# Where a wide up-projection's product is transposed, and the rate of wide pieces near the end of a feed-forward block

## The chip, the cores and the metric

The kernel runs on one core of one Trainium2 chip. It is timed in device microseconds (us) of one execution. A core has TensorE (PE; its weight loads are listed apart as PEld), VectorE (DVE), ScalarE (ACT), GpSimd (POOL) and SyncE (SP), which here only issues DMAs. Each engine works through its own queue in order.

## What is computed

Two layers of a decoder trunk on 256 tokens of width 2048, in float32. Each layer has an attention block and then a gated feed-forward block with a layer norm after it. The change touches the feed-forward blocks alone:

```python
SEQ = 256; D_MODEL = 2048; DEPTH = 2; D_FF = 5632

def swiglu(x, w_gate, w_up, w_down):
    return (jax.nn.silu(x @ w_gate) * (x @ w_up)) @ w_down
...
    x = layer_norm(DEEPNORM_ALPHA * x + y, ln_g[layer, 0], ln_b[layer, 0])
    y = swiglu(x, w_gate[layer], w_up[layer], w_down[layer])
    x = layer_norm(DEEPNORM_ALPHA * x + y, ln_g[layer, 1], ln_b[layer, 1])
```

## The kernel before

Float32 products are made of three matmuls each: every operand is split into a high part (`XH`, `wh`, `sh`) and a rest (`XL`, `wl`, `sl`), and high times high, high times rest and rest times high are summed in PSUM.

**Chunks and pieces.** The weights come as chunks of 512 columns, and a chunk as pieces of 256 rows by 512 columns (512 KB). `D_FF` gives 11 blocks of columns, f = 0 to 10. `g0_9` is the gate chunk of layer 0 and block 9, `u0_8` the up chunk of block 8, and `d0_3_2` the third of four down chunks that take in blocks 6 and 7. A chunk of the gate or of up has 8 pieces, and this down chunk has 4. `visits` is the list of pieces in the order in which PE works through them; one entry is a visit. Both layers have the same list.

**Plain and wide pieces.** A plain piece is 12 matmuls of 512 columns. Its load goes to one of four `raw` buffers, ACT writes the high part (line 422) and DVE the rest (line 424). Gate chunks from block 2 on, and the up chunk of block 8 (`UPS`), are wide (`c.S`): `emit_s` multiplies them by a Strassen-like scheme, in 21 matmuls of 256 columns (lines 448 to 450) that read three sums of blocks of the piece. So the split of a wide piece (`split_s`) is longer: three pre-sums on DVE in the raw buffer (lines 380, 382, 383), the high part `sh` on ACT (line 386), the rest `sl` on DVE (line 389). There are two raw buffers for wide pieces (`sraw_92`, `sraw_93`), and two pairs of split buffers (`sh_102` with `sl_103`, `sh_104` with `sl_105`). The raw buffer is free for the next load when line 389 has read it; the pair of split buffers is free when PE has done the piece. The high part and the rest are not put in the queues with the pre-sums: they are owed (`owe`, `pay`), and go in behind a later split.

**The order.** `ffn_part` lays out the plain visits and puts the wide ones between them at a rate: `want` grows by 0.53 per plain visit from the tenth on, and by 0.7 from number 118 on, which is near the end of `u0_7`. After each visit `feed_more` takes in the next splits as buffers allow, in the order of the pieces. When a wide chunk is done, `drain_s` gathers its four accumulators: one pass on ACT (line 478) and five on DVE (lines 479 to 484). For up of block 8, DVE then multiplies by the gate (line 1089).

**Transposes.** The product of block f has to be transposed before the down chunks can use it: `h_T` puts four transposes of 128x128 in one PSUM bank (line 597), twice (t = 0 and 1), and ACT and DVE move each bank to `YH` and `YL` (lines 113 and 114). `after_up[layer, f]` says after which two visits. From block 2 on the banks come from `PAIRS`: the plain chunk in work holds one pair, and the transposes take a bank of the other pair, which the plain chunk before held and the next one will hold. A down chunk's two banks are read by line 928.

Of the kernel before, what the change touches and what calls it, by code (L numbers as in the profile page):

```python
# [53 lines left out]
def trunk_kernel(ctx: ExitStack, tc: tile.TileContext, x, ab_w_in, b_f, ab_w_out,  # L54
# [67 lines left out]
    visits = []  # L122
    chunks = {}

    def add_chunk(name, xs, kslots, srcs, tags=None):
        subs = []
        o = 0
        for n in srcs[0]:
            subs.append((n, o))
            o += n  # L130
        c = Chunk(name, xs, kslots, subs, srcs[1], tags or ("mm",) * len(subs))
        c.n = o
        chunks[name] = c
        return c

    def kmajor(c, hs=None):
        for h in (range(c.nh) if hs is None else hs):
            visits.append((c, h, (0, 1)))
# [18 lines left out]
    def lead_begin(c):  # L157
        for t in (0, 1):
            for h in range(LEAD):
                visits.append((c, h, (t,)))  # L160
        kmajor(c, range(LEAD, c.nh))

    def rows(w, k0, cols):
        return [(o, n, w[k0:k0 + 256, c0:c0 + n].rearrange("(k p) c -> p k c", p=P))
                for o, n, c0 in cols]
# [37 lines left out]
    after_up = {}  # L203
    win = {}

    def ffn_part(layer):
        def wide(nm, w, f):
            return add_chunk(f"{nm}{layer}_{f}", "X", K16, ([512], lambda h: rows(
                w[layer], h * 256, [(0, 512, f * 512)])))

        def down(gi):
            grp = GROUPS[gi]
            slots = [4 * (f % 4) + k for f in grp for k in range(4)]
            for n in range(4):
                c = add_chunk(f"d{layer}_{gi}_{n}", "Y", slots, (
                    [512], lambda h, n=n: rows(
                        w_down[layer], grp[0] * 512 + h * 256, [(0, 512, n * 512)])))
                if gi == len(GROUPS) - 1 and n == 3:
                    (lead_final if layer == 1 else lead_end)(c)
                else:  # L220
                    kmajor(c)

        g0 = wide("g", w_gate, 0)
        g0.pair = 0
        lead_begin(g0)
        base = len(visits)
        for f in range(NF):
            if f == 1:
                kmajor(wide("g", w_gate, 1))
            c = wide("u", w_up, f)  # L230
            if f in UPS:
                c.S = True
            else:
                kmajor(c)
            if f in (1, 3, 5, 7):
                down(f // 2)
        down(len(GROUPS) - 1)
        flat = visits[base:]
        del visits[base:]
        ends = {}  # L240
        for f in range(NF):
            if f not in UPS:
                e = ends[f] = max(k for k, v in enumerate(flat) if v[0].name == f"u{layer}_{f}")
                o = e + 2 - f % 2
                after_up[layer, f] = [(v[0].name, v[1], v[2]) for v in flat[o:o + 3]]
        gates = []
        for f in range(len(PLAIN), NF):
            c = wide("g", w_gate, f)
            c.S = True
            gates += [(c, h, (0, 1)) for h in range(8)]  # L250
            if f in UPS:
                gates += [(chunks[f"u{layer}_{f}"], h, (0, 1)) for h in range(8)]
        near = {ends[f] + 2 for f in (1, 3, 5, 7, 9)}
        ns, want = 0, 0.0
        for k, v in enumerate(flat):
            visits.append(v)
            want = max(want + (0 if k < 9 else 0.53 if k < 118 else 0.7),
                       ns + 1 if k in near else 0)
            while ns < min(len(gates), int(want)):
                visits.append(gates[ns])  # L260
                ns += 1
                c = gates[ns - 1][0]
                f = int(c.name[3:])
                if ns % 8 == 0 and c.name[0] == "g" and f not in UPS:
                    assert k < ends[f] - 1, (k, ns, ends)
        assert ns == len(gates)
        for f in UPS:
            e = max(k for k, v in enumerate(visits) if v[0].name == f"u{layer}_{f}")
            after_up[layer, f] = [(v[0].name, v[1], v[2]) for v in visits[e + 1:e + 3]]

    w_out_part("oa", ab_w_out[0])
    ffn_part(0)
    wi = mla_w_in[0]
    c = add_chunk("m0", "X", K16, ([512], lambda h: rows(wi, h * 256, [(0, 512, 0)])))
# [8 lines left out]
    for nm in order:  # L283
# [8 lines left out]
        kmajor(c)  # L292
    w_out_part("om", mla_w_out[0])
    ffn_part(1)


# [1161 lines left out]
```

## Time and profile before

| | |
|---|---|
| three runs | 2169.24, 2170.62 (median), 2171.04 us |
| the profiled execution | 2170.17 us, its span 2168.3 us |
| PE busy | 2131.5 us, 98% of the span |
| DVE busy | 1639.8 us, 76% |
| ACT busy | 1046.3 us, 48% |
| DMA | 410.39 MB, mean 189 GB/s |
| mean granted TensorE clock | 0.994 |

The span runs from the first instruction to the last; some 1.9 us of the execution lie around it. PE's share is that of modelled ends, so a busy PE isn't yet a PE at its best pace: the start of one matmul to the start of the next tells more. An idle time in brackets is that of the instruction's engine just before it, with what ended it.

### The profile page before, as it was taken

Reading aid. Unit: us, or ns where it says so; the run is one execution under the profiler, and the core shown is the slowest. Engines: PE = TensorE matmul, PEld = TensorE weight load, DVE = VectorE, ACT = ScalarE, POOL = GpSimd, SP = SyncE. Lnnn points to the kernel's source line nnn. Section 1 sums busy time; section 2 is a strip of 40 time slices with the busy share of each in tenths; the row PEclk is TensorE's granted clock in tenths of the full one; section 3 lists DMA queues with packets and bytes.
Section 4 is the critical chain, followed back from the end, with each engine's and each line's share of the span. In section 5 each row is a group of like instructions: output and inputs, shape, how many; then the busy total and the mean of one; then the engine's idle time right before and its main releaser. Section 6 shows DMA issues by size and latency. Waiting matters only on the chain.

```text
span 2168.3 us, 31334 instructions
## 1 busy us (share of the span) xinstructions
PE 2131.5 (98%) x12426; PEld 1865.3 (86%) x12426; DVE 1639.8 (76%) x2117; ACT 1046.3 (48%) x1210; POOL 94.5 (4%) x142
## 2 busy tenths in 40 slices
PE   9999999999999999989999999999999999999998
PEld 9899998788888888878878998878888888887886
DVE  5555656788888888888866676598887888888875
ACT  5444544455444454444534665355544444454451
POOL 2100000100000000000001330010000000000000
PEclk9999999999999999999999999999999999999999
DMA  8565556555565555555765544745654555555582
GB/s 287 170 206 165 172 185 216 192 184 190 169 208 191 194 194 189 183 184 173 258 214 163 176 133 143 274 139 182 204 195 165 187 198 189 198 166 173 200 282 78
DMA packets 230338, 410.39 MB, mean 189 GB/s; under 512 B 14088, under 2 KB 58160, under 8 KB 229168
## 3 DMA queue, kind: packets, MB, share of 16 engines
q1 hardware_dynamic: 230192, 408.40, 56.5%
q8 instruction: 97, 1.59, 0.3%
q14 instruction: 49, 0.40, 0.1%
HBM read 402.56 MB, written 5.78 MB: 188 GB/s over the span
## 4 chain that ended last, share of the span: by engine, by line
PE 59%; issue 35%; DVE 3%; DMA 1%; POOL 1%; ACT 1%; SPq 0%; DVEq 0%; POOLq 0%; ACTq 0%
PE mm L117 12%; PE mm L118 12%; PE mm L119 12%; PE mm L507 3%; PE mm L509 3%; PE mm L511 3%; PE tp L597 2%; PE att L119 1%; PE att L118 1%; PE att L117 1%; PE sA L449 1%; PE sB L449 1%; PE sC L449 1%; PE sC L450 1%; PE sB L448 1%
## 5 line engine op out<-in xcount | busy, mean ns | idle before, releaser
L422 ACT ACTIVATE wh<-raw 128x1024 fp32r<-128x1024 f32 (+3 forms) x424 | 443.0, 1048 | 576.5 <-PE mm L119 358.2
L424 DVE TENSOR_TENSOR wl<-raw,wh 128x1024 fp32r<-128x1024 f32 (+3 forms) x424 | 511.5, 1211 | 193.0 <-ACT wh L422 186.4
L389 DVE TENSOR_TENSOR sl<-sraw,sh 128x1792 fp32r<-128x1792 f32 x160 | 323.5, 2022 | 37.6 <-ACT sh L386 37.4
L117 PE MATMUL mm<-wh,XH 128*128 128x512 f32 (+3 forms) x896 | 350.1, 391 | 0.0
L118 PE MATMUL mm<-wl,XH 128*128 128x512 f32 (+3 forms) x896 | 346.7, 387 | 0.0
L119 PE MATMUL mm<-wh,XL 128*128 128x512 f32 (+3 forms) x896 | 346.0, 386 | 0.0
L117 PE MATMUL mm<-wh,YH 128*128 128x512 f32 (+1 forms) x768 | 306.8, 400 | 11.3 <-DVE YL L114 10.7
L118 PE MATMUL mm<-wl,YH 128*128 128x512 f32 (+1 forms) x768 | 304.7, 397 | 0.0
L119 PE MATMUL mm<-wh,YL 128*128 128x512 f32 (+1 forms) x768 | 304.4, 396 | 0.0
L386 ACT ACTIVATE sh<-sraw 128x1792 fp32r<-128x1792 f32 x160 | 270.3, 1689 | 13.6 <-DVE sraw L383 10.6
L119 PEld LDWEIGHTS mm<-wh,XL 128*128 128x128 f32 x896 | 168.1, 188 | 36.6
L117 PEld LDWEIGHTS mm<-wh,XH 128*128 128x128 f32 x896 | 168.6, 188 | 31.2
L118 PEld LDWEIGHTS mm<-wl,XH 128*128 128x128 f32 x896 | 168.3, 188 | 30.6
L117 PEld LDWEIGHTS mm<-wh,YH 128*128 128x128 f32 x768 | 145.6, 190 | 43.4 <-DVE YL L114 11.4
L119 PEld LDWEIGHTS mm<-wh,YL 128*128 128x128 f32 x768 | 145.2, 189 | 35.2
L118 PEld LDWEIGHTS mm<-wl,YH 128*128 128x128 f32 x768 | 145.4, 189 | 30.7
L380 DVE TENSOR_TENSOR sraw<-sraw 128x512 f32<-128x512 f32 x160 | 109.5, 685 | 12.3 <-DMA sraw<-in_ffn_w_gate_dram 11.8
L507 PE MATMUL mm<-XH,wh 128*128 128x256 f32 x364 | 104.0, 286 | 0.0
L509 PE MATMUL mm<-XH,wl 128*128 128x256 f32 x364 | 102.3, 281 | 0.0
L511 PE MATMUL mm<-XL,wh 128*128 128x256 f32 x364 | 102.2, 281 | 0.0
L448 PE MATMUL sA<-sh,XH 128*128 128x256 f32 x320 | 92.1, 288 | 0.0
L449 PE MATMUL sA<-sl,XH 128*128 128x256 f32 x320 | 89.9, 281 | 1.8 <-DVE sl L389 1.8
(302 smaller groups left out, 4254.2 us busy)
## 6 DMA issues: line engine op xcount, KB each, us to landing
raw<-in_ffn_w_down_dram SPq DMA_DIRECT2D x160, 512.0 KB, 5.5
raw<-in_ffn_w_up_dram SPq DMA_DIRECT2D x155, 512.0 KB, 4.8
sraw<-in_ffn_w_gate_dram SPq DMA_DIRECT2D x149, 512.0 KB, 3.9
raw<-in_ab_w_in_dram SPq DMA_DIRECT2D x80, 256.0 KB, 3.1
raw<-in_ffn_w_gate_dram SPq DMA_DIRECT2D x27, 512.0 KB, 4.5
sraw<-in_ab_w_in_dram SPq DMA_DIRECT2D x48, 256.0 KB, 3.3
raw<-in_ab_w_out_dram SPq DMA_DIRECT2D x22, 512.0 KB, 3.5
sraw<-in_ffn_w_up_dram SPq DMA_DIRECT2D x21, 512.0 KB, 4.0
```

Source lines behind the costliest of these rows:

```text
L117: nc.tensor.matmul(o, lh, rh, start=start, stop=False)
L118: nc.tensor.matmul(o, lh, rl, start=False, stop=False)
L119: nc.tensor.matmul(o, ll, rh, start=False, stop=stop)
L386: nc.scalar.activation(sh, r[:, 256:2048], AF.Copy)
L389: nc.vector.tensor_tensor(sl, r[:, 256:2048], sh.bitcast(F32), op=ALU.subtract)
L422: nc.scalar.activation(wh[:, a:b], r[:, a:b], AF.Copy)
L424: nc.vector.tensor_tensor(wl[:, a:b], r[:, a:b], wh[:, a:b].bitcast(F32), op=ALU.subtract)
L448: nc.tensor.matmul(o, h, w[0][:, q], start=first, stop=False)
L449: nc.tensor.matmul(o, h, w[1][:, q], start=False, stop=False)
L507: nc.tensor.matmul(o, wh[:, kk, a:a + P], XH[:, slot, :], start=first, stop=False)
L509: nc.tensor.matmul(o, wl[:, kk, a:a + P], XH[:, slot, :], start=False, stop=False)
L511: nc.tensor.matmul(o, wh[:, kk, a:a + P], XL[:, slot, :], start=False, stop=last)
```

## The change

Two edits in `ffn_part`. The rate of wide pieces from plain visit 118 on is 0.74 and not 0.7. And `after_up` of block 8, whose up chunk is wide, is taken from the plain visits behind the last piece of that chunk: the first of them that begins a chunk, and the one behind that. Before it was the next two visits, of whatever kind.

```diff
-            want = max(want + (0 if k < 9 else 0.53 if k < 118 else 0.7),
+            want = max(want + (0 if k < 9 else 0.53 if k < 118 else 0.74),
                        ns + 1 if k in near else 0)
             while ns < min(len(gates), int(want)):
                 visits.append(gates[ns])
...
         for f in UPS:
             e = max(k for k, v in enumerate(visits) if v[0].name == f"u{layer}_{f}")
-            after_up[layer, f] = [(v[0].name, v[1], v[2]) for v in visits[e + 1:e + 3]]
+            rest = [v for v in visits[e + 1:] if not v[0].S]
+            o = next(k for k, v in enumerate(rest) if v[1] == 0)
+            after_up[layer, f] = [(v[0].name, v[1], v[2]) for v in rest[o:o + 2]]
```

The visits from the second piece of `u8` on, in either layer, a wide one by its name (u8.1 is piece 1 of `u0_8` or `u1_8`) and a plain one as p:

```
before: u8.1 p u8.2 p p u8.3 p u8.4 p u8.5 p p u8.6 p u8.7 p p g9.0 p g9.1 p p g9.2 p g9.3 p g9.4 p p g9.5 p g9.6 p p g9.7 p g10.0 p p g10.1 p g10.2 p g10.3 p p g10.4 p g10.5 p p g10.6 p g10.7 p p
after:  u8.1 p u8.2 p u8.3 p u8.4 p p u8.5 p u8.6 p p u8.7 p g9.0 p g9.1 p p g9.2 p g9.3 p g9.4 p p g9.5 p g9.6 p g9.7 p p g10.0 p g10.1 p g10.2 p p g10.3 p g10.4 p g10.5 p g10.6 p p g10.7 p p p p
```

The two plain visits behind u8.7 are `d0_3_1` piece 3 and `d0_3_2` piece 0 in both. Before, the transposes stand behind these two. After, they stand behind `d0_3_2` pieces 0 and 1. Up to u8.2 the two lists are the same, and so they are behind the last row above. The same instructions run, in both layers; only their order is another. Lines of the changed kernel from 269 on are two higher.

PE at the first transposes of `u8`'s product, before (`mm_7982` is a bank of `d0_3_1`, `mm_8116` one of `d0_3_2`, `tp` the bank of the transposes, `gt` the product):

```order
L119 MATMUL mm_7982<-wh_96,YL 128x512
L597 MATMUL tp_8103<-ident,gt_3529 128x128 x4
L117 MATMUL mm_8116<-wh_98,YH 128x512
L118 MATMUL mm_8116<-wl_99,YH 128x512
L119 MATMUL mm_8116<-wh_98,YL 128x512
```

The same place after (`mm_8137` is a bank of `d0_3_2`, `sA_8106` an accumulator of `g0_9`):

```order
L119 MATMUL mm_8137<-wh_98,YL 128x512
L599 MATMUL tp_8150<-ident,gt_3529 128x128 x4
L450 MATMUL sA_8106<-sh_104,XH 128x256
L451 MATMUL sA_8106<-sl_105,XH 128x256
L452 MATMUL sA_8106<-sh_104,XL 128x256
```

The transposes stood between the end of one down chunk and the start of the next. Now they stand behind the first piece of that next chunk, and piece 1 of `g0_9` follows.

DVE behind the last piece of `u8`, before (the first row is the last of the drain; `sl_103<-sraw_93` is the rest of g9.0, the pre-sums on `sraw_92` belong to g9.1, the two rows of line 928 read `d0_3_1`):

```order
L484 TENSOR_TENSOR xt_3526<-xt_3526,sC_7690 128x2x256
L1089 TENSOR_TENSOR gt_3529<-gt_3529,xt_3526 128x1024
L380 TENSOR_TENSOR sraw_92<-sraw_92 128x512
L382 TENSOR_TENSOR sraw_92<-sraw_92 128x256
L383 TENSOR_TENSOR sraw_92<-sraw_92 128x256
L389 TENSOR_TENSOR sl_103<-sraw_93,sh_102 128x1792
L424 TENSOR_TENSOR wl_95<-raw_91,wh_94 128x1024
L928 TENSOR_TENSOR X_3525<-X_3525,mm_7981 128x512
L928 TENSOR_TENSOR X_3525<-X_3525,mm_7982 128x512
L114 TENSOR_TENSOR YL<-tp_8103,YH 128x4x128
```

And after:

```order
L486 TENSOR_TENSOR xt_3526<-xt_3526,sC_7689 128x2x256
L1091 TENSOR_TENSOR gt_3529<-gt_3529,xt_3526 128x1024
L382 TENSOR_TENSOR sraw_92<-sraw_92 128x512
L384 TENSOR_TENSOR sraw_92<-sraw_92 128x256
L385 TENSOR_TENSOR sraw_92<-sraw_92 128x256
L391 TENSOR_TENSOR sl_103<-sraw_93,sh_102 128x1792
L426 TENSOR_TENSOR wl_101<-raw_90,wh_100 128x1024
L426 TENSOR_TENSOR wl_95<-raw_91,wh_94 128x1024
L391 TENSOR_TENSOR sl_105<-sraw_92,sh_104 128x1792
L930 TENSOR_TENSOR X_3525<-X_3525,mm_7980 128x512
L930 TENSOR_TENSOR X_3525<-X_3525,mm_7981 128x512
```

The rest of g9.0 keeps its place behind the drain, while PE's visit of g9.0 comes one plain piece earlier. One more plain split and the rest of g9.1 stand ahead of the two rows that free `d0_3_1`'s banks; line 114 comes later.

DVE from the rest of g10.4 (`sl_103<-sraw_93`) to that of g10.5 (`sl_105<-sraw_92`), before; line 114 belongs to transposes:

```order
L389 TENSOR_TENSOR sl_103<-sraw_93,sh_102 128x1792
L424 TENSOR_TENSOR wl_97<-raw_88,wh_96 128x1024
L114 TENSOR_TENSOR YL<-tp_8725,YH 128x4x128
L424 TENSOR_TENSOR wl_99<-raw_89,wh_98 128x1024
L389 TENSOR_TENSOR sl_105<-sraw_92,sh_104 128x1792
```

The same stretch after; line 1087 multiplies `u9` by its gate, and the pre-sums on `sraw_93` are those of g10.6:

```order
L391 TENSOR_TENSOR sl_103<-sraw_93,sh_102 128x1792
L426 TENSOR_TENSOR wl_101<-raw_90,wh_100 128x1024
L1087 TENSOR_TENSOR gt_3530<-gt_3530,mm_8440 128x512
L1087 TENSOR_TENSOR gt_3530<-gt_3530,mm_8441 128x512
L382 TENSOR_TENSOR sraw_93<-sraw_93 128x512
L384 TENSOR_TENSOR sraw_93<-sraw_93 128x256
L385 TENSOR_TENSOR sraw_93<-sraw_93 128x256
L391 TENSOR_TENSOR sl_105<-sraw_92,sh_104 128x1792
```

The rest of g10.5 now stands behind the pre-sums of g10.6, which work in the buffer that the rest of g10.4 has just read. The visits of g10.4 and g10.5 have one plain piece between them in both lists.

## Rows read from the trace of the kernel before

**Rows 1.** The page: busy time, share of the span and instructions of each engine.

```profile
PE 2131.5 (98%) x12426; PEld 1865.3 (86%) x12426; DVE 1639.8 (76%) x2117; ACT 1046.3 (48%) x1210; POOL 94.5 (4%) x142
```

**Rows 2.** Who waited for whom on PE: us in total, times, longest us.

```profile
PE mm L117 <- DVE YL L114: 10.7, 2, 5.7
...
PE sA L449 <- DVE sl L389: 1.8, 4, 0.8
```

**Rows 3.** The timeline of PE, layer 0: start us, us, instruction, count [idle before].

```profile
960.11 0.39 PE L117 MATMUL mm<-wh,YH 128*128 128x512 f32 x1
...
963.00 0.66 PE L597 MATMUL tp<-ident,gt 128*128 128x128 f32 x4
...
969.38 0.80 PE L117 MATMUL mm<-wh,YH 128*128 128x512 f32 x1 [5.73 <-DVE YL L114]
...
974.35 0.60 PE L597 MATMUL tp<-ident,gt 128*128 128x128 f32 x4
...
974.71 0.36 PE L448 MATMUL sA<-sh,XH 128*128 128x256 f32 x1
```

**Rows 4.** The timeline of DVE over the same wait.

```profile
958.97 0.42 DVE L479 TENSOR_TENSOR xt<-xt,sD 128x256 f32<-128x256 f32 x1
...
961.72 1.22 DVE L1089 TENSOR_TENSOR gt<-gt,xt 128x1024 f32<-128x1024 f32 x1
...
964.38 2.02 DVE L389 TENSOR_TENSOR sl<-sraw,sh 128x1792 fp32r<-128x1792 f32 x1
...
966.31 1.22 DVE L424 TENSOR_TENSOR wl<-raw,wh 128x1024 fp32r<-128x1024 f32 x1
...
967.45 1.28 DVE L928 TENSOR_TENSOR X<-X,mm 128x512 f32<-128x512 f32 x2
```

**Rows 5.** The timeline of PE at the same place of layer 1.

```profile
1973.49 0.65 PE L597 MATMUL tp<-ident,gt 128*128 128x128 f32 x4
...
1984.45 0.37 PE L448 MATMUL sA<-sh,XH 128*128 128x256 f32 x1
```

**Rows 6.** Timelines of DVE, SP and PE: g10.1's rest, the load behind it, g10.2.

```profile
1029.65 2.02 DVE L389 TENSOR_TENSOR sl<-sraw,sh 128x1792 fp32r<-128x1792 f32 x1
...
1031.69 0.37 SPq L358 DMA_DIRECT2D sraw<-in_ffn_w_gate_dram  x1
...
1035.74 0.69 DVE L380 TENSOR_TENSOR sraw<-sraw 128x512 f32<-128x512 f32 x1 [2.94 <-DMA sraw<-in_ffn_w_gate_dram]
...
1037.26 2.02 DVE L389 TENSOR_TENSOR sl<-sraw,sh 128x1792 fp32r<-128x1792 f32 x1
...
1039.33 0.39 PE L449 MATMUL sA<-sl,XH 128*128 128x256 f32 x1 [0.31 <-DVE sl L389]
```

**Rows 7.** The timeline of DVE: two rests with two plain splits between them.

```profile
936.70 2.02 DVE L389 TENSOR_TENSOR sl<-sraw,sh 128x1792 fp32r<-128x1792 f32 x1
...
940.90 2.02 DVE L389 TENSOR_TENSOR sl<-sraw,sh 128x1792 fp32r<-128x1792 f32 x1
```

**Rows 8.** Timelines of DVE and PE: u8.1's rest, then u8.1, a plain piece, u8.2.

```profile
916.23 2.02 DVE L389 TENSOR_TENSOR sl<-sraw,sh 128x1792 fp32r<-128x1792 f32 x1
...
919.65 0.28 PE L449 MATMUL sA<-sl,XH 128*128 128x256 f32 x1
...
922.02 0.40 PE L117 MATMUL mm<-wh,XH 128*128 128x512 f32 x1
...
924.93 0.28 PE L449 MATMUL sA<-sl,XH 128*128 128x256 f32 x1
```

**Rows 9.** PE's timeline at two other waits; last, a stretch's busy us by engine, PEclk.

```profile
660.66 0.66 PE L597 MATMUL tp<-ident,gt 128*128 128x128 f32 x4 [2.36 <-DVE gt L1085]
...
1667.60 1.12 PE L597 MATMUL tp<-ident,gt 128*128 128x128 f32 x4 [2.96 <-DVE gt L1085]
...
1667.60:1673.50 5.90, 5.90 (x27) 5.80 (x28) 5.83 (x7) 1.66 (x2) 0.00 (x0) 0.50 0.90 296
```

**Rows 10.** DMA issues: count, KB each, median us from issue to landing.

```profile
sraw<-in_ffn_w_gate_dram SPq DMA_DIRECT2D x149, 512.0 KB, 3.9
```

## The prediction

> **What bounds the kernel now.** The page says that PE is busy for 98% of the span [rows 1], so a time is won or lost by what PE waits for. The table of PE's waits comes next: the longest entry is two waits of 10.7 us in all, one in each layer, of a plain matmul for line 114 [rows 2]. The timeline shows the place [rows 3]. The transposes of `u8`'s product run at 963.00, in a bank that the next down chunk takes over. That chunk's first matmul can't start until ACT and DVE have emptied the bank, and it starts at 969.38. DVE isn't idle there: from 958.97 to 968.73 it drains `u8`, multiplies, makes pre-sums, a rest and a split, and adds the down chunk's two banks [rows 4], and line 114 stands behind all that. The matmuls after the wait also run slowly, 0.80 and not 0.39 us [rows 3].
>
> The third view is that of the wide pieces' splits. PE wants `sl` at a wide piece's second matmul (line 449); in the whole run it waits for it four times, 1.8 us together [rows 2]. How close this is, one place shows [rows 6]. The rest of g10.1 begins at 1029.65 and frees its raw buffer. SP issues the next load into it 2.04 later, DVE waits 2.94 us for that load and can begin the pre-sums at 1035.74. Only behind them stands the rest of g10.2, from 1037.26 on; PE waits for it and goes on at 1039.33. So where a rest stands in DVE's queue directly behind pre-sums in the buffer that the rest before has freed, the two rests lie 7.61 us apart. I call this a slow link. Where two plain splits and nothing else stand between two rests, they lie 4.20 us apart [rows 7]: a quick link.
>
> **PE's side of it.** From u8.1's second matmul to u8.2's, with one plain piece between, PE takes 5.28 us [rows 8]: 2.37 for the rest of the wide piece and 2.91 for the plain one and the first wide matmul. A wide matmul starts 0.12 behind the one before (2.37 for 20), so a plain piece is 2.79, and with two plain pieces between it is 8.07. Four transposes add 0.36 (974.35 to 974.71) [rows 3]. A slow link thus fits over two plain pieces (0.46 to spare) and not over one (2.33 short); a quick link gains 1.08 over one. In the order before, a slow link falls on a single plain piece three times in a layer (u8.4, g9.3, g10.2), each time with leads saved up behind it, and only the last one shows a wait. The new rate packs wide pieces as one, one, two plain between them, and then it falls so seven times: u8.2, u8.3, g9.3, g9.6, g10.1, g10.4, g10.5.
>
> **What the change takes away.** In layer 0 PE needs 11.71 us from the transposes at 963.00 to the wide piece at 974.71, for work of 0.36 + 2.79 + 0.36 = 3.51: 8.2 lost [rows 3]. In layer 1 it is 10.96, so 7.45 lost [rows 5]. Both go, as no chunk starts right behind these transposes any more. With the 0.3 at g10.2 in either layer [rows 6], 16.3 us go.
>
> **What it brings at g9.0.** DVE's queue is the same there: drain, multiplication, pre-sums, rest of g9.0. That rest begins at 964.38, ends 2.02 later, and PE has it 0.05 after [rows 4, 6]: 966.45. But g9.0 now comes behind one plain piece and not two. PE begins that piece at 960.11 [rows 3], so it wants the rest at 960.11 + 2.79 + 0.12 = 963.02, and waits 3.43. The drain follows PE's last matmul of `u8` and not the queue ahead of it, so this wait moves with PE. Queued behind it on PE are the first piece of `d_3_2` and the transposes. These then come at 966.45 + 2.37 + 2.79 = 971.6. DVE will have emptied the old banks by then: from 966.31 on, two splits of 1.14, a rest of 1.93 and the two rows of line 928 end at 971.8, the first of the two near 971.2 [rows 4]. At most 0.2 is lost, since one of the two banks is the later one. The transposes themselves, ACT's and DVE's rows for them and all loads are the same in number and cost nothing new.
>
> **What it brings elsewhere.** I go along the wide pieces with the lead, the time by which a rest is ready before PE wants it. New lead = old lead + PE's time − link; below zero PE waits and the lead is 0. At u8.1, up to which both orders agree, the rest ends at 918.25, is ready at 918.30 and wanted at 919.65: lead 1.35 [rows 8].
> u8.2: 1.35 + 5.28 − 7.61, a wait of 0.98. u8.3, transposes ahead: 5.64 − 7.61, a wait of 1.97. Then quick and slow links over single and double gaps build a lead of 3 until u8.7, and g9.0 waits 3.43 as above. g9.1: quick, with transposes, lead 1.44; g9.2: 2.26 (transposes and two plain pieces); g9.3: a wait of 0.07. g9.4: 1.08; g9.5: 1.54; g9.6: a wait of 0.79. g9.7: 1.08.
> g10.0 stands behind the drain of g9. Counted from PE's second matmul of g9.7, the rest of g9.7 ended at −1.13. Behind it come the two rows of line 928 (1.2), pre-sums (1.52 [rows 6]) and a split (1.14), so the drain begins near +2.6. From drain to end of rest took 7.43 for `u8` [rows 4]; the same is my estimate here, where passes on ACT replace the multiplication. It is ready near +10.1 and wanted at +8.07: a wait of 2.0. Then g10.1 waits 2.33; g10.2 leads by 1.08 and g10.3 by 1.54; g10.4 waits 0.79 and g10.5, with transposes, 1.97. Sum of a layer: 0.98 + 1.97 + 3.43 + 0.07 + 0.79 + 2.0 + 2.33 + 0.79 + 1.97 = 14.3; both layers 28.7.
>
> **The clock.** Behind an idle time of 2.36 us PE ran on at full pace; behind one of 2.96 it was granted 0.50, the lower of its levels (1.2 GHz), for 5.9 us, which costs 2.95 [rows 9]. At g9.0 I count on the drop (3.3 idle), and on none at the others (2.3 at most). While PE is slow, DVE gains the same 2.95 of lead, which does away with the waits at g9.3 and g9.6 and with some 1.5 of that at g10.0. About 0.5 a layer stays, 1.1 in all.
>
> **The sum.** −16.3 + 28.7 + 1.1 = +13.5 us. The profiled execution took 2170.17, of which the span is 2168.3; the median of three runs is 2170.62. So 2183.7 by the one and 2184 by the other. Tails: the link is the term that counts. At 7.2 us the same walk gives 10.2 a layer, so 2176; at 7.9 each of the seven waits behind slow links grows by 0.3 and the leads ahead of them shrink by as much, so 2190, and a drop of the clock at one more wait makes it 2193.
>
> **Rivals.**
> *The loads land sooner.* If a load for a wide piece took 0.85 us less than the 4.05 from issue to use in [rows 6], a slow link would be 6.76. The walk gives 0.13 + 1.12 + 3.43 + 0.6 (g10.0 can't be readier than the end of PE's g9.7 lets it) + 1.48 + 0.2 = 7.0 a layer, 14.0 in all, which with the clock's 1.1 is 1.2 less than what goes: 2169, no change. For it speaks that only one such wait stands in my rows; against it, that the median of 149 such loads is 3.9 [rows 10], so 4.05 isn't a rare one. Chance 0.08. The Trainium skill (DMA: Bandwidth & Descriptors, "Anatomy of one DMA — SWDGE (gpsimd) path") gives about 2.0 us fixed and the bytes at 436 GB/s for a DMA that GpSimd issues; for 512 KB that would be an estimate of 3.2 us, and this rival's time. The rows here, of loads that SP issues, don't agree: 3.9.
>
> *The loads hide altogether.* If the load behind a rest were no part of the link, because the buffer is free long before DVE comes to the pre-sums, split, pre-sums and rest would be 1.14 + 1.52 + 1.93 = 4.6 and fit under 5.28. Only g9.0 and 0.6 at g10.0 would wait, 8.1 in all against 16.3: 2162 with the clock up, 2168 with it down at g9.0. That is the faster side, and it decides from a link of 5.28 downward. Against it stands the order, where the pre-sums use the buffer number of the rest just before. Chance 0.05.
>
> *The clock drops at more waits.* Waits of 2.0 to 2.3 lie just under the 2.36 that left the clock up. A drop at u8.3 in both layers is 5.9 that nothing gives back before g9.0, whose wait moves with PE: 2190. Chance 0.07.
>
> **How the numbers follow.** The forecast, 2176 to 2194 around 2184, has 0.80. The range 2175 to 2194 leaves out the two rivals below and some tail. A measurement of this kernel tells about 0.2% (4.3 us) from no change. Slower by more than that: the forecast but for 0.01, and the clock's rival, 0.86. Within: the first rival, half of the second and that tail, 0.10. Faster: 0.04.
>
> **What would show it.** Right: no wait of line 117 for line 114 in the changed profile; PE's waits for `sl` (now line 391) near 25 to 30 us in some 16 to 18 places, longest 3.3 at g9.0; DVE's waits for `sraw` loads at line 382 grown to several of 2 us and more. The two stretches from u8.1 to the last wide piece would each be 6 to 7 us longer, all else equal to 0.1. Wrong: waits for `sl` under 10 us in all, or a gap of under 7 us between rests at slow links, would end the forecast; a wait of PE's transposes for line 930 of more than 1 us would mean that the banks come free later than I walked.

## The result, and the profile after

The changed kernel takes 2182.9 us (median of four runs, 2180.9 to 2187.1) and the kernel before 2169.9 in the same set: a ratio of 1.0062, 95% interval 1.0044 to 1.0079. It is slower by about 13 us, where the prediction had 13.5. Its profiled execution took 2184.32 us, of which 2182.5 are the span.

The first line of the page, which answers to [rows 1], shows how little shares of busy time tell: DVE does the same work (1640.1 us) and PE is as "busy" as before.

```profile
PE 2136.6 (98%) x12426; PEld 1869.2 (86%) x12426; DVE 1640.1 (75%) x2117; ACT 1045.0 (48%) x1210; POOL 94.5 (4%) x142
```

The table of waits does tell. Of PE's waits in the changed kernel (who waits for whom, us in total, times, longest), these lines answer to [rows 2]:

```profile
PE sA L451 <- DVE sl L391: 22.2, 15, 3.6
...
PE mm L117 <- DVE X L930: 0.5, 2, 0.3
```

The line `mm L117 <- DVE YL L114` with its 10.7 us is gone, and no line of `tp` waiting for line 930 has come. In its place PE waits 22.2 us for rests of wide pieces, where it waited 1.8. Of line 930 only two plain matmuls behind the block wait, for 0.5.

The timeline of PE at the old place of the wait, layer 0 (start us, us, instruction, count, idle before), answers to [rows 3]:

```profile
972.61 0.39 PE L451 MATMUL sA<-sl,XH 128*128 128x256 f32 x1 [3.63 <-DVE sl L391]
...
979.38 0.60 PE L599 MATMUL tp<-ident,gt 128*128 128x128 f32 x4
...
979.74 0.36 PE L450 MATMUL sA<-sh,XH 128*128 128x256 f32 x1
```

From the transposes to the wide piece behind them PE now needs 0.36 us, so the bank costs nothing any more. But one plain piece earlier, at g9.0, PE stood idle for 3.63.

A slow link in the changed kernel, between the rests of u8.2 and u8.3 (timelines of DVE, SP and PE), answers to [rows 6]:

```profile
926.57 2.02 DVE L391 TENSOR_TENSOR sl<-sraw,sh 128x1792 fp32r<-128x1792 f32 x1
...
928.61 0.37 SPq L360 DMA_DIRECT2D sraw<-in_ffn_w_up_dram  x1
928.64 0.38 PE L451 MATMUL sA<-sl,XH 128*128 128x256 f32 x1 [0.92 <-DVE sl L391]
...
932.72 0.69 DVE L382 TENSOR_TENSOR sraw<-sraw 128x512 f32<-128x512 f32 x1 [1.80 <-DMA sraw<-in_ffn_w_up_dram]
...
934.25 2.02 DVE L391 TENSOR_TENSOR sl<-sraw,sh 128x1792 fp32r<-128x1792 f32 x1
...
936.32 0.39 PE L451 MATMUL sA<-sl,XH 128*128 128x256 f32 x1 [1.70 <-DVE sl L391]
```

The first rest ends, SP issues the next load 2.04 after its start, DVE waits for that load and can use it 4.11 after the issue, and the second rest follows 7.68 after the first. One plain piece lies between the two wide ones, and PE is idle before both.

### The profile page after: what moved, and what is told of

Read it like the earlier page. It is cut to its first block, busy times and chain, and to the rows that moved or that the text cites. A ratio compares the mean times of both kernels' runs of the same rounds, so it can differ in the third digit from the quotient of the medians.

```text
span 2182.5 us, 31338 instructions
## 1 busy us (share of the span) xinstructions
PE 2136.6 (98%) x12426; PEld 1869.2 (86%) x12426; DVE 1640.1 (75%) x2117; ACT 1045.0 (48%) x1210; POOL 94.5 (4%) x142
## 4 chain that ended last, share of the span: by engine, by line
PE 57%; issue 35%; DVE 4%; DMA 1%; POOL 1%; ACT 1%; SPq 0%; DVEq 0%; POOLq 0%; ACTq 0%
PE mm L117 11%; PE mm L118 11%; PE mm L119 11%; PE mm L509 3%; PE mm L513 3%; PE mm L511 3%; PE tp L599 1%; PE att L118 1%; PE att L119 1%; PE att L117 1%; DVE sl L391 1%; PE sA L451 1%; PE sA L452 1%; PE sB L451 1%; PE sB L450 1%
## 5 line engine op out<-in xcount | busy, mean ns | idle before, releaser
L424 ACT ACTIVATE wh<-raw 128x1024 fp32r<-128x1024 f32 (+4 forms) x427 | 445.5, 1046 | 619.3 <-PE mm L119 349.9
L426 DVE TENSOR_TENSOR wl<-raw,wh 128x1024 fp32r<-128x1024 f32 (+4 forms) x427 | 514.6, 1210 | 193.0 <-ACT wh L424 184.6
L391 DVE TENSOR_TENSOR sl<-sraw,sh 128x1792 fp32r<-128x1792 f32 x160 | 323.6, 2023 | 39.6 <-ACT sh L388 39.4
L117 PE MATMUL mm<-wh,XH 128*128 128x512 f32 (+3 forms) x888 | 347.3, 391 | 0.0
L117 PE MATMUL mm<-wh,YH 128*128 128x512 f32 (+1 forms) x768 | 303.9, 396 | 0.0
L388 ACT ACTIVATE sh<-sraw 128x1792 fp32r<-128x1792 f32 x160 | 270.2, 1689 | 12.6 <-DVE sraw L385 12.4
L117 PEld LDWEIGHTS mm<-wh,XH 128*128 128x128 f32 x888 | 167.5, 189 | 31.0
L117 PEld LDWEIGHTS mm<-wh,YH 128*128 128x128 f32 x768 | 144.6, 188 | 30.5
L382 DVE TENSOR_TENSOR sraw<-sraw 128x512 f32<-128x512 f32 x160 | 109.7, 686 | 37.9 <-DMA sraw<-in_ffn_w_gate_dram 28.3
L451 PE MATMUL sA<-sl,XH 128*128 128x256 f32 x320 | 91.4, 286 | 22.3 <-DVE sl L391 22.2
```

The lines of the kernel that those rows point to most:

```text
L117: nc.tensor.matmul(o, lh, rh, start=start, stop=False)
L388: nc.scalar.activation(sh, r[:, 256:2048], AF.Copy)
L391: nc.vector.tensor_tensor(sl, r[:, 256:2048], sh.bitcast(F32), op=ALU.subtract)
L424: nc.scalar.activation(wh[:, a:b], r[:, a:b], AF.Copy)
L426: nc.vector.tensor_tensor(wl[:, a:b], r[:, a:b], wh[:, a:b].bitcast(F32), op=ALU.subtract)
L451: nc.tensor.matmul(o, h, w[1][:, q], start=False, stop=False)
```

## The experiments

Each run is a kernel of its own; "before" is the kernel before, run on the same chip beside them. Ratios are to it, with 95% intervals.

| run | rate | transposes | rest of blocks 8 to 10 | us | ratio |
|---|---|---|---|---|---|
| before | 0.70 | old place | behind pre-sums | 2171.8 | |
| the change | 0.74 | new place | behind | 2182.9 (its own set) | 1.0062 (1.0044 to 1.0079) |
| rate_alone | 0.74 | old place | behind | 2189.8 | 1.0086 (1.0072 to 1.0099) |
| transposes_alone | 0.70 | new place | behind | 2163.0 | 0.9964 (0.9952 to 0.9977) |
| half_load | 0.74 | new place | behind, half the load | 2171.6 | 1.0006 (0.9997 to 1.0015) |
| rest_first | 0.74 | new place | ahead of pre-sums | 2163.9 | 0.9968 (0.9956 to 0.9980) |
| rest_first_before | 0.70 | old place | ahead | 2168.8 | 0.9989 (0.9980 to 0.9998) |
| rate_072 | 0.72 | new place | behind | 2177.0 | 1.0029 (1.0019 to 1.0039) |
| one_later | 0.70 | one piece later | behind | 2160.6 | 0.9949 (0.9936 to 0.9961) |
| later_rest_first | 0.70 | one piece later | ahead | 2155.1 | 0.9928 (0.9914 to 0.9941) |

**Which of the two edits costs?** First the rate alone, on the kernel before:

```diff
-            want = max(want + (0 if k < 9 else 0.53 if k < 118 else 0.7),
+            want = max(want + (0 if k < 9 else 0.53 if k < 118 else 0.74),
```

> The kernel before with the new rate alone; the transposes stay at the two visits behind the last piece of u8. Theory (slow links: a rest behind pre-sums whose load waits for the rest before): the pattern of wide pieces is that of the changed kernel, so its waits for sl come, 10 to 12 us a layer. And the bank is still wanted too early: the second pair of transposes now has piece 0 of g9 behind it and then the first matmul of the next down chunk, so a wait of line 117 for line 114 stays, some 3 to 4 us a layer. Sum: about -10.7 + 7 + 24 less 2 saved elsewhere, 2186 to 2190, slower than the changed kernel. Rival A (the new place of the transposes is what costs): within 4 us of 2170. Rival B (the clock alone makes the loss): waits for sl under 10 us in all, and stretches at half clock longer than before by 10 us or more.

2189.8: the theory's time, and rival A is out by far. PE's waits in that run:

```profile
PE sA L449 <- DVE sl L389: 20.0, 15, 3.2
...
PE mm L117 <- DVE YL L114: 3.4, 2, 2.0
```

The waits for `sl` come whole with the rate. Two sizes were off. The waits for line 114 came to 3.4 in all and not to 7. The half clock took more than I had thought (in this run the mean granted clock is 0.992, against 0.994 before); here is one stretch of layer 1, right behind one of the waits for line 114. The columns are the stretch, its length, busy us of PE, PEld, DVE, ACT and POOL (instructions), granted clock, DMA share and GB/s:

```profile
1998.90:2002.20 3.30, 3.30 (x10) 2.55 (x9) 3.23 (x6) 1.71 (x2) 0.00 (x0) 0.50 0.21 81
```

So rival B has a share, as a follower of the waits and not instead of them.

Then the place of the transposes alone, at the rate of before:

```diff
-            after_up[layer, f] = [(v[0].name, v[1], v[2]) for v in visits[e + 1:e + 3]]
+            rest = [v for v in visits[e + 1:] if not v[0].S]
+            o = next(k for k, v in enumerate(rest) if v[1] == 0)
+            after_up[layer, f] = [(v[0].name, v[1], v[2]) for v in rest[o:o + 2]]
```

> The kernel before with the new place of the transposes alone, rate 0.7. Theory: the two waits of line 117 for line 114 (10.7 us, and 15.7 with the slow matmuls behind) go, and in their place the transposes wait for line 930, which empties the banks of the old down chunk: DVE ended that at 968.73 in the kernel before, the first bank near 968.1, and PE comes to the transposes 2.8 after 963.0. That is 2.3 to 3.9 in either layer, 4.6 to 7.8 in all. Nothing else changes: 2160 to 2165, faster than before. If the lower clock follows the new waits, up to 2170. Rival A (the new place of the transposes is what costs in the changed kernel): 2178 or more. Waits for sl stay near the 1.8 us of before.

2163.0, faster than before: this half of the change is good by itself. Its waits:

```profile
PE tp L599 <- DVE X L930: 5.8, 2, 2.9
...
PE sA L451 <- DVE sl L391: 1.3, 2, 0.8
```

The old wait of 10.7 has turned into one of 5.8 for another step of DVE's queue, line 930, which empties the bank. Alone the edits give 1.0086 and 0.9964, together 1.0062: the rate costs 19 us and the place brings 8. On top of the rate the place is worth only 5, as no more than 3.4 of the old wait is left there. Not all of the 5 is in the waits: those for `sl` and for line 114 are 23.4 in rate_alone and 22.2 in the changed kernel, and in the one trace of each the rest goes with the granted clock, 0.992 against 0.994.

**Is the load a link of the chain?** The changed kernel with half of each late wide load:

```diff
-            for k in ((slice(0, 1), slice(1, 2)) if halves else (slice(0, 2),)):
+            top = c.S and c.name.split("_")[1] in ("8", "9", "10")
+            for k in ((slice(0, 1),) if top else (slice(0, 1), slice(1, 2)) if halves else (slice(0, 2),)):
```

> The changed kernel, but of each wide piece of blocks 8 to 10 only the upper 128 of 256 rows are loaded (256 KB and not 512); the other half of the buffer keeps old data, so this leaves out loads and nothing else, and engines do the same work in the same order. Theory: the load is a link in the chain from rest to rest, so a shorter load shortens every wait behind a slow link (u8.2, u8.3, g9.6, g10.1, g10.4, g10.5) by as much as it lands sooner, while the waits at g9.0 and g10.0, which stand behind drains, stay. If the load lands 0.5 to 1.0 us sooner, 5 to 11 us go: 2172 to 2178. Rival (the loads are not what DVE waits for; the order of splits or the clock is): within 3 us of 2183.

2171.6, some 12 us less than the changed kernel (1.0062 to 1.0006), just below the range that I had expected. By the median the loads got shorter by 1.2 us, more than the 0.5 to 1.0 of my estimate: 4.0 for whole ones and 2.8 for half ones in one trace. The rows are those of PE's matmul by `sl` (count | busy us, mean ns | idle before, what ended most of it) and of the loads (count, KB, median us from issue to landing):

```profile
L452 PE MATMUL sA<-sl,XH 128*128 128x256 f32 x320 | 91.2, 285 | 12.1 <-DVE sl L392 12.1
...
sraw<-in_ffn_w_gate_dram SPq DMA_DIRECT2D x101, 512.0 KB, 4.0
...
sraw<-in_ffn_w_gate_dram SPq DMA_DIRECT2D x48, 256.0 KB, 2.8
```

And the same link as above, u8.2 to u8.3, in this run:

```profile
924.59 2.02 DVE L392 TENSOR_TENSOR sl<-sraw,sh 128x1792 fp32r<-128x1792 f32 x1
...
926.63 0.34 SPq L361 DMA_DIRECT2D sraw<-in_ffn_w_up_dram  x1
...
929.96 0.69 DVE L383 TENSOR_TENSOR sraw<-sraw 128x512 f32<-128x512 f32 x1 [1.03 <-DMA sraw<-in_ffn_w_up_dram]
...
931.49 2.02 DVE L392 TENSOR_TENSOR sl<-sraw,sh 128x1792 fp32r<-128x1792 f32 x1
...
933.56 0.38 PE L452 MATMUL sA<-sl,XH 128*128 128x256 f32 x1 [0.79 <-DVE sl L392]
```

From issue to use 3.33 and not 4.11, from rest to rest 6.90 and not 7.68: the link shrinks by the same 0.78 as the time from issue to use, and the wait at u8.3 by 0.91. DVE's queue and work are the same. This shows directly that the load stands in the chain. Where the rest follows a drain, at g9.0, PE waits as long as in the changed kernel (3.63 in layer 0).

**Does another order of DVE's queue do without the load?** The changed kernel, with one step moved:

```diff
-                new = split_s(j)
+                first = c.name.split("_")[1] in ("8", "9", "10")
+                new = None if first else split_s(j)
                 for o in owed:
                     o["age"] += 1
                 pay("act")
                 pay("dve")
-                owe(j, *new)
+                owe(j, *(new or split_s(j)))
```

> The changed kernel, but for wide pieces of blocks 8 to 10 the owed high part and rest of the piece before go into the queues ahead of the next piece's pre-sums, not behind them. Theory: this takes the load out of the chain from rest to rest. The waits at u8.2, u8.3, g9.6, g10.1, g10.5 go, that at g9.0 falls by the 1.5 of the pre-sums to about 2, and at the transposes some 1 to 2 us for line 930 may come; waits for sl 6 to 9 us in all where the changed kernel has 22. 2163 to 2169, 14 to 20 less than the changed kernel and no slower than the kernel before. Rival A (too little of DVE's time is left near the end at this rate, whatever its order): still 2178 or more. Rival B (DVE then waits for ACT's high part in place of the load): waits of DVE's rests for sh of 10 us or more, 2175 or more.

2163.9, 20 us less than the changed kernel. Timelines of DVE and SP where the slow link stood (rests of u8.1, u8.2 and u8.3, and the loads behind them):

```profile
916.70 2.02 DVE L391 TENSOR_TENSOR sl<-sraw,sh 128x1792 fp32r<-128x1792 f32 x1 [0.37 <-ACT sh L388]
...
918.76 0.37 SPq L360 DMA_DIRECT2D sraw<-in_ffn_w_up_dram  x1
...
922.15 2.02 DVE L391 TENSOR_TENSOR sl<-sraw,sh 128x1792 fp32r<-128x1792 f32 x1 [0.77 <-ACT sh L388]
924.10 0.68 DVE L382 TENSOR_TENSOR sraw<-sraw 128x512 f32<-128x512 f32 x1
...
927.95 2.02 DVE L391 TENSOR_TENSOR sl<-sraw,sh 128x1792 fp32r<-128x1792 f32 x1
```

The load is issued at 918.76, and its pre-sums begin at 924.10 without any idle time: it now lands beside a plain split and a rest. The links are 5.45 and 5.80 and not 7.68. DVE's and PE's waits of that run:

```profile
DVE sl L391 <- ACT sh L388: 55.0, 116, 2.7
...
DVE sraw L382 <- DMA sraw<-in_ffn_w_gate_dram: 2.6, 3, 1.2
```

```profile
PE sA L452 <- DVE sl L391: 6.6, 9, 1.8
...
PE tp L600 <- DVE X L931: 1.5, 1, 1.5
```

In the changed kernel the first two lines were 39.4 and 28.3:

```profile
DVE sl L391 <- ACT sh L388: 39.4, 96, 1.2
DVE sraw L382 <- DMA sraw<-in_ffn_w_gate_dram: 28.3, 17, 3.1
```

So rival B's wait did come, 15.6 us more of DVE for ACT, but not its time: DVE's waits for the loads of the gate fell by 25.7. Rival A falls too: at this rate DVE has enough time, its order was at fault. At g9.0 PE waits 1.76 in place of 3.63, which is the 1.5 of the pre-sums and a little more. The wait of the transposes for the emptying of the banks (line 931 here) came once, with 1.5.

The same edit on the kernel before:

> The kernel before with the one edit of rest_first: in blocks 8 to 10 the owed rest of a wide piece goes ahead of the next piece's pre-sums. Theory (a slow link costs only where it falls on one plain piece without a lead, which in the kernel before it does once in a layer, for 0.3; its loss is the bank of the transposes): the 10.7 of line 117 behind line 114 stays, some 5 to 6 in either layer, and only 1 to 4 us go: 2166 to 2171. Rival (this order of DVE's queue is better by itself, whatever the packing of the pieces): as much is gained as in rest_first, 15 us or more, 2156 or less.

2168.8, 3 us less than before, and the wait for the bank is what it was. The order of the queue isn't worth much in itself; it matters where the pieces are packed too closely for the slow link.

```profile
PE mm L117 <- DVE YL L114: 10.7, 2, 5.7
```

**Does the loss follow the list of pieces?** The changed kernel with a rate of 0.72:

> The changed kernel at a rate of 0.72. Its list of pieces is that of the changed kernel up to g9.3, and then two plain pieces stand between g9.3 and g9.4, g9.6 and g9.7, g10.0 and g10.1. Theory: waits at u8.2, u8.3, g9.0 and g10.0 stay (about 1.0, 1.9, 3.5, 1.5 to 2), those at g10.1, g10.4 and g10.5 of some 2.1, 0.4 to 1.0 and up to 2.0 go: 16 to 18 in all against 22.2, and so 2176 to 2180 by the waits alone, down to 2174 if a stretch at half clock less follows. Rival A (each wide piece that is pulled forward costs alike): half of the way from 0.70 (2163, the run transposes_alone) to 0.74 (2183), so 2173. Rival B (g9.0's new place behind one plain piece is the whole loss): still 2183.

2177.0, in the theory's range. Rival A's half way would be a ratio of 1.0013, which is outside the interval; rival B's 2183 is a ratio of 1.0062, outside too. The waits:

```profile
PE sA L451 <- DVE sl L391: 14.6, 10, 3.6
PE tp L599 <- DVE gt L1087: 8.5, 6, 2.9
```

The waits for `sl` are 7.6 us less than in the changed kernel, and 14.6 is under the 16 to 18 that I had expected. Those at g10.1, g10.4 and g10.5 went as forecast. The one at g10.0 was to stay and went too, and g10.2 waits 0.78 and 0.41 in its place. I had not foreseen that 2.6 comes back on the second line: in either layer one set of transposes of `u9`'s product now comes too soon behind the multiplication that it reads (1.11 and 0.70), and one place of layer 1 far ahead of `u8` waits 1.03 in place of 0.18. So the time came out in the theory's range with two misses in its parts that partly offset each other.

**A version that beats both.** The wait of 5.8 in transposes_alone asks for a place one plain piece later:

```diff
-            after_up[layer, f] = [(v[0].name, v[1], v[2]) for v in rest[o:o + 2]]
+            after_up[layer, f] = [(v[0].name, v[1], v[2]) for v in rest[o + 1:o + 3]]
```

> The run transposes_alone (rate 0.7, new place) with the transposes of block 8 one plain piece later, at pieces 1 and 2 of that down chunk. Theory: the wait of 2.9 us in either layer of the transposes for line 930 goes, since DVE empties the banks within the 2.8 to 5.2 of the piece more; of these 5.8, half comes back as waits for sl at g9.0 and g9.7, which that wait had given a lead: 2160 to 2162, 1 to 3 less than transposes_alone. Rival (the wait is hidden slack, and DVE's queue is the bound here): the whole 5.8 comes back, 2163.

2160.6. The line of transposes waiting for line 930 is gone with its 5.8, and waits for `sl` are 4.8 and not 1.3. So 3.5 came back, somewhat more than the half expected. It came at g9.0 (0.5 in either layer), as expected, but otherwise at g9.3 (1.21 and 1.01) and not at g9.7:

```profile
PE sA L451 <- DVE sl L391: 4.8, 7, 1.2
```

With the rest ahead of the pre-sums as well:

> one_later with the edit of rest_first too: rate 0.7, transposes one plain piece later, rest ahead of pre-sums in blocks 8 to 10. Theory: what slow links and the drain still cost at g9.0 and g9.7 in one_later goes as well, waits for sl under 3 us in all: 2155 to 2159, below both kernels and below all other runs. Rival (at rate 0.7 no slow link costs anything, and the earlier rest only delays the drain or the emptying of the banks): 2160 or more.

2155.1, 0.72% below the kernel before (0.59 to 0.86) and the fastest of all. Its waits for `sl`, below those of the kernel before:

```profile
PE sA L452 <- DVE sl L391: 1.4, 4, 0.5
```

## Why the prediction was right, step by step

**What goes: right.** The wait for line 114 is gone in both layers, and the transposes cost 0.36 again. The run transposes_alone shows this half by itself.

**What comes: most places and the sum right.** Waits of PE at the second matmul of a wide piece, from start to start against the usual pace, so each is 0.1 to 0.3 us longer than the idle time that the profile gives:

| piece | predicted | layer 0 | layer 1 |
|---|---|---|---|
| u8.2 | 0.98 | 1.08 | 0.91 |
| u8.3 | 1.97 | 1.95 | 1.92 |
| g9.0 | 3.43 | 3.79 | 3.44 |
| g9.3, g9.6 | 0.07, 0.79 | 0 | 0 |
| g10.0 | 2.0 | 1.15 | 1.94 |
| g10.1 | 2.33 | 1.98 | 2.13 |
| g10.4 | 0.79 | 0 | 1.01 |
| g10.5 | 1.97 | 0.39 | 1.98 |
| sum | 14.3 | 10.3 | 13.3 |

Ahead of the clock the sum was 28.7, and less what half clock gives DVE as leads (2.4 a layer) 23.9; measured are 23.6. The walk's one link of 7.61 was about right: at the seven places, in both layers, rest to rest took 7.29 to 7.77 us. How the sum splits was less well seen. The leads did away with the waits at g9.3 and g9.6, as predicted, but not with 1.5 at g10.0, which in layer 1 kept its 1.94. And layer 0 has 3 us less than layer 1. Of that, 0.8 is at g10.0. Most of the rest lies behind g10.1, where PE ran at half clock once more in layer 0, from 1034.6 on: that gave DVE some 1.7 of lead, and the three links from g10.2 to g10.5 were 1.3 shorter there than in layer 1 (21.9 against 23.3 in all). The term at g10.0 was right in layer 1 but not for the reason given: in both layers DVE comes to the rest 1.20 us before ACT's high part is done, and that one stands in ACT's queue behind line 1082, which works on the drained `g9`. From layer 1, DVE and ACT:

```profile
2039.65 2.03 DVE L391 TENSOR_TENSOR sl<-sraw,sh 128x1792 fp32r<-128x1792 f32 x1 [1.20 <-ACT sh L388]
```

```profile
2036.96 1.06 ACT L1082 ACTIVATE gt<-gt 128x1024 f32<-128x1024 f32 x1 [4.09 <-DVE gt L486]
2037.93 1.69 ACT L388 ACTIVATE sh<-sraw 128x1792 fp32r<-128x1792 f32 x1
```

**The clock: right that it drops at g9.0, wrong in length, and one more.** Stretches of the changed kernel; the first two are behind the wait at g9.0 of layer 1, the third behind that at g10.1 of layer 0, the fourth behind that at u8.3:

```profile
1986.95:1990.30 3.35, 3.35 (x17) 3.35 (x17) 3.35 (x3) 0.00 (x0) 0.00 (x0) 0.50 0.75 219
1990.40:1993.50 3.10, 3.10 (x17) 2.51 (x17) 3.03 (x7) 1.06 (x1) 0.00 (x0) 1.00 0.67 226
1034.65:1038.00 3.35, 3.35 (x18) 3.35 (x18) 3.33 (x3) 1.69 (x2) 0.00 (x0) 0.50 0.84 270
936.40:939.80 3.40, 3.40 (x25) 3.23 (x26) 2.91 (x3) 3.13 (x3) 0.00 (x0) 1.00 0.69 222
```

The half clock lasted some 3.4 us and not 5.9, so each drop costs 1.7 and not 2.95. The 5.9 was read off a long drop [rows 9], and the one behind the old wait of 5.73 was long too: 0.50 for 6.70 us from 967.20 on in the kernel before. Those of the changed kernel in the two stretches were short; why, no run shows. There were three there and not two, 5.1 in all. That gives −16.3 + 23.6 + 5.1 = +12.4 for the two stretches. Measured from u8.1's second matmul to the second transposes behind g10.7, the last wide piece, layer 0 took 169.30 before (919.65 to 1088.95) and 174.38 after (922.29 to 1096.67); layer 1 took 168.62 (1929.96 to 2098.58) and 175.93 (1936.99 to 2112.92). That is +5.1 and +7.3, 12.4 in all, as worked out. The prediction's sum was 13.5 with 5.9 for the clock.

```profile
1088.95 0.38 PE L597 MATMUL tp<-ident,gt 128*128 128x128 f32 x2
...
2098.58 0.38 PE L597 MATMUL tp<-ident,gt 128*128 128x128 f32 x2
```

```profile
922.29 0.28 PE L451 MATMUL sA<-sl,XH 128*128 128x256 f32 x1
...
1096.67 0.38 PE L599 MATMUL tp<-ident,gt 128*128 128x128 f32 x2
...
2112.92 0.27 PE L599 MATMUL tp<-ident,gt 128*128 128x128 f32 x1
```

**The signs.** No wait of line 117 for line 114 is left, and none of the transposes for line 930 has come, as foretold. PE's waits for `sl` are 22.2 us in 15 places, the longest 3.63 at g9.0, where the prediction asked for 25 to 30 in 16 to 18 and 3.3: its own sum less the leads, 23.9, lay under that already. 12 of the 15 places, with 21.0 us, lie in the two stretches. The stretches grew by 5.1 and 7.3, where 6 to 7 each was foretold.

**The rivals.** "The loads land sooner" and "the loads hide altogether" fall by the trace after: from issue to use 4.11, and 28.3 us of DVE waiting for those of the gate, where it was 11.8 before. The run half_load shows that the first would have had its effect, had the loads been that short: with 3.33 from issue to use the loss was gone. "The clock drops at more waits" came true once in the two stretches, for 1.7, but not at u8.3, which had been its place.

**Luck in it.** That the clock's two errors (each drop shorter, one drop more) nearly cancel was not foreseen. And the span grew by 14.2 and not 12.4. From the start to u8.1's second matmul the profiled execution took 922.29 us and the one before 919.65; of these 2.6 the half clock told of below is the part that can be named. Between the two stretches it got 0.7 back, and that is a balance, with two differences of the clock outside the stretches in it: a drop came behind a wait of 1.74 at 1221.56, and the long one at 1667.60 of the kernel before [rows 9] did not come, though the same transposes waited 2.93. The medians lie 13.0 apart.

## What to carry to other kernels

Where a buffer goes round between two queues (a rest frees it, a load fills it, pre-sums wait for it), ask what else stands behind that wait in the in-order queue; moving the ready step ahead of the waiting one was worth 20 us here, and nothing of the work changed. On the kernel before, where the pieces are packed less closely, the same move was worth 3. A rate that packs pieces closer can be judged by a walk along them with one lead and two link lengths from the trace; it found the places, and most of the sizes, of the waits that came in the two stretches; how the half clock would shift them it found less well. When a wait is removed, look for what else of the same queue the moved step waits for, as transposes_alone shows: 10.7 became 5.8, and one place later 0, of which 3.5 came back as waits for `sl`.

## What the hardware showed that I had not expected

The length of an idle time alone doesn't decide whether the clock falls. The same transposes of layer 0 waited 2.36 us in the profiled execution before [rows 9] and 2.37 after. Behind them the clock stayed at 1.00 before:

```profile
661.40:664.70 3.30, 3.30 (x26) 3.12 (x25) 3.30 (x3) 0.55 (x1) 0.00 (x0) 1.00 1.01 335
```

and went to 0.50, the lower of its two levels (1.2 GHz), after:

```profile
661.79 0.65 PE L599 MATMUL tp<-ident,gt 128*128 128x128 f32 x4 [2.37 <-DVE gt L1087]
```

```profile
662.60:665.90 3.30, 3.30 (x18) 3.30 (x17) 3.30 (x3) 0.48 (x1) 0.00 (x0) 0.50 0.99 343
```

In rest_first a wait of only 1.76 brought it down in layer 0, and the same wait of 1.76 at the same place of layer 1 left it up:

```profile
966.48 0.39 PE L452 MATMUL sA<-sl,XH 128*128 128x256 f32 x1 [1.76 <-DVE sl L391]
...
1972.33 0.38 PE L452 MATMUL sA<-sl,XH 128*128 128x256 f32 x1 [1.76 <-DVE sl L391]
```

```profile
967.80:971.10 3.30, 3.30 (x15) 3.11 (x14) 3.30 (x4) 1.70 (x1) 0.00 (x0) 0.50 0.87 303
...
1973.70:1977.00 3.30, 3.30 (x21) 2.90 (x20) 3.30 (x4) 1.71 (x1) 0.00 (x0) 1.00 0.86 309
```

So an order between the waits that "leave it up" and those that "bring it down", as the prediction drew it from [rows 9], isn't borne out: at g10.1 of the changed kernel an idle time of 1.82 in layer 0 brought it down, and one of 1.97 in layer 1 left it up. What these traces give is a price for each short drop, 1.7 us where it lasted 3.4; what decides on a drop stays open. The spread from run to run goes with the mean granted clock: the four runs of the changed kernel took 2180.9, 2181.5, 2184.3 and 2187.1 us at 0.996, 0.997, 0.994 and 0.992. Four runs don't show that the one makes the other.
